# GpSimd in place of VectorE for two groups of low-part subtractions in a hybrid encoder block

## The chip, the core and the metric

The kernel runs on one core of a Trainium2 chip (trn2). The metric is the device time of one execution in microseconds (us), the median of several runs. The engines are TensorE (PE; its weight loads are listed apart as PEld), VectorE (DVE), ScalarE (ACT), GpSimd (POOL) and SyncE (SP, which here only issues DMAs). Each engine executes its own instructions in the order in which they were written into its queue.

## The reference

One layer of an encoder over 16 meta tokens and 2048 tokens of width 1024. A projection feeds two groups, attention (4 query heads, 2 key/value heads, rotary positions) and a Fourier mix; both are normalised, projected back and added, and a squared-ReLU MLP follows. What the change touches belongs to the Fourier group:

```python
def fourier_mix(u, w_f):
    b, l, _ = u.shape
    ug = u.reshape(b, l, N_FOURIER_GROUPS, FOURIER_GROUP_W)
    f = jnp.fft.fft2(ug, axes=(1, 3), norm='ortho').real
    y = jnp.einsum('blgc,gcd->blgd', f, w_f)
    return y.reshape(b, l, FOURIER_W)
...
    mixed = jnp.concatenate([rms_norm(attn, g_attn_out[i]), rms_norm(four, g_fourier_out[i])], axis=-1)
    h = h + mixed @ w_out[i]
```

## The kernel before

**Three products for one.** Nearly every large product is made of three matmuls on numbers that are split in two: `hi` is a rounded copy (written by ACT) and `lo` is what is left (`x - hi`, a subtraction on DVE). `Split` (L70 to L74) issues the two, and `mm3` (L80, L81, L82) multiplies hi by hi, hi by lo and lo by hi into one PSUM bank. So a line L70 or L71 in the profile is a split, and L80 to L82 are matmuls; the names of the tiles tell of what.

**Stages.** First the projections and their rotary and transposing work (to about 310 us), then the Fourier transform interleaved with the first attention units, then the Fourier half of the output projection interleaved with further attention units (to about 590 us), then the attention half of the output projection and the MLP with the rest of the attention.

**The Fourier transform** (`fourier`, `transform`, `load_tables`). The transform over the tokens is four products with tables of cosines and sines, `tr` 0 to 3; 0 and 1 give the even frequencies, 2 and 3 the odd ones. For each `tr`, `load_tables` (L528) loads raw tables `traw` of 128 x 516 numbers by DMA (three buffers), ACT copies each to `thi` (L548) and DVE subtracts to `tlo` (L551). The even transforms have two whole tables each, the odd ones four, so there are 12 `tlo` subtractions, 8 of them for `tr` 2 and 3. `transform` multiplies the channels by a small matrix (`pa`, L570), splits the result (`ahi`, `alo`), and its `product` makes `py`. Results are combined by DVE into two long tiles, `EV` and `UA`.

**The Fourier half of the output projection** (`out_f`). For each of 16 tiles `t` of 128 tokens, `rows(t)` gathers a tile's 128 columns from `EV` and `UA` in two interleaved halves (one tile has four pieces instead of two, so 34 pieces in all, nearly all 128 x 256 numbers, every second element of the tile): a split into `yh` and `yl` (L926, which the profile lists under L70 and L71), and a square into `ysq` on ACT (L927). GpSimd adds the squares up (`ysq`, L929, two additions a tile); `scale` sums them over the channels by a small matmul (`pys`), and DVE and GpSimd make the factor `rs_f` of it (L190, L192). Then 24 matmuls make `pof`, two banks of 12, and DVE adds each, scaled, into `xo` (L957).

**Attention beside it** (`attention`). A unit is 512 query columns. `scores` makes 17 products `s` of three matmuls; ACT copies them to tiles `S` (L773) and DVE keeps a running maximum `M` (L776, L779, L781, L768); transposes `pm_m` (L787) and `pd_m` (L796) on PE turn it into `mb`. `softmax` subtracts `mb` on DVE (L832), ACT takes the exponential (L833), DVE sums in `acc` (L837, L839) and splits each half to `ph` and `pl` (L71); PE multiplies by the values into `o`, three matmuls a split: `ph`, then `pl`, then `ph` again. The first two units multiply unsplit numbers (L842). GpSimd's queue issues the DMAs of queries `q`, keys `kt` and values `vt`.

**What sets the order.** The program is written as interleaved generators (`mix`, `with_weights`), and a scheduler then orders each engine's instructions by its own estimate of when their inputs are ready. Where an instruction moves to another engine, the order of all the others in that stretch is found anew.

Of the kernel before, what the change touches and what calls it, by code (L numbers as in the profile page):

```python
# [14 lines left out]
ALU = mybir.AluOpType  # L15
# [41 lines left out]
def f32v(ap):  # L57
    return ap.bitcast(F32)
# [18 lines left out]
def mm3(nc, out, a, b, first, last, chain=False):  # L77


    nc.tensor.matmul(out, a[0], b[0], start=first, stop=False, skip_group_check=chain)  # L80
    nc.tensor.matmul(out, a[0], b[1], start=False, stop=False, skip_group_check=chain)  # L81
    nc.tensor.matmul(out, a[1], b[0], start=False, stop=last, skip_group_check=chain)  # L82
# [53 lines left out]
def encoder_block(ctx: ExitStack, tc: tile.TileContext, x, meta, w_in, w_f,  # L136
                  w_out, w_up, w_down, g_fin, g_cols, g_rows, c_id, c_rope, c_dft, c_even, c_odd, c_rem, out):
    nc = tc.nc
    split = Split(nc)
# [9 lines left out]
    def bank(name, shape=(P, 512)):  # L149
        return mmp.tile(list(shape), F32, name=name, tag="mm")  # L150
# [36 lines left out]
    def rstd_of(pool, ss, n, width, tag, rows=P):  # L187

        ms = pool.tile([P, n], F32, name="ms_" + tag, tag="ms_" + tag, bufs=2 if pool is tp else 4)
        nc.vector.tensor_scalar(ms[:rows], ss, 1.0 / width, EPS, op0=ALU.mult, op1=ALU.add)  # L190
        rs = pool.tile([P, n], F32, name="rs_" + tag, tag="rs_" + tag, bufs=2 if pool is tp else 4)
        nc.gpsimd.tensor_tensor(rs[:rows], ms[:rows], mhalf[:rows, :n], op=ALU.pow)  # L192
        return rs
# [331 lines left out]
    def sources(tr):  # L525
        full, rest = ROWS[tr]
        return (EV, UA, EV, UA)[tr], full, rest, len(full) // 2 if tr < 2 else len(full)

    def load_tables(tr):

        src, full, rest, n_tab = sources(tr)
        rem = ft.tile([P, NG, REM], F32, name=f"rem{tr}", tag="rem", bufs=1)
        nc.vector.memset(rem, 0.0)
        for o in (0, 32, 64):
            for lo, hi in rest:
                nc.vector.tensor_copy(rem[:, :, o:o + hi - lo], src[:, :, lo:hi])
                o += hi - lo
        tabs = []
        for nt in list(range(n_tab)) + [len(full)]:
            rows = P if nt < n_tab else REM  # L540
            raw = ft.tile([P, TW], F32, name=f"traw{tr}_{nt}", tag="traw", bufs=3)
            nc.sync.dma_start(raw[:rows], (c_even[tr, nt] if tr < 2 else c_odd[tr - 2, nt]) if rows == P else c_rem[tr])
            raw = raw.rearrange("p (c n) -> p c n", c=2)
            hi = ft.tile([P, 2, CHP], R32, name=f"thi{tr}_{nt}", tag="thi", bufs=T_BUFS[1])[:, :, :CH]
            with ExitStack() as behind:
                for i in last_acts:
                    behind.enter_context(tc.issue_after(i))
                nc.scalar.copy(hi[:rows], raw[:rows])  # L548
                if rows == P:
                    lo = ft.tile([P, 2, CHP], R32, name=f"tlo{tr}_{nt}", tag="tlo", bufs=T_BUFS[0])[:, :, :CH]  # L550
                    nc.vector.tensor_tensor(lo, raw, f32v(hi), op=ALU.subtract)  # L551
                    tabs.append((hi, lo))
                else:
                    nc.vector.tensor_tensor(hi[32:64], raw[32:64], f32v(hi[32:64]), op=ALU.subtract)
                    tabs.append(hi)
        tables[tr] = tabs, rem

    def transform(tr):

        src, full, rest, n_tab = sources(tr)  # L560
        if tr not in tables:
            load_tables(tr)
# [32 lines left out]
    for j in range(LAST + 1):  # L595
# [16 lines left out]
        else:  # L612
            if j == 1:
                chan_dft()
            if j == LAST:
                for _ in proj_u(j):
                    side()
                spread_m()
                for src in (EV, UA):
                    for g in range(NG):  # L620
                        fold(src, g)
                    for g in range(0, NG, 2):
                        fold_even(src, g)
                wu.release()
                ft = Lines(tc.alloc_tile_pool(name="ft", bufs=1, reuse_waits="tile"), small)
                load_tables(0)
# [20 lines left out]
    def y_runs(par, e0, e1):  # L647

        m, t0, o0, t1, o1 = YO if par else YE
        got = []  # L650
        if e0 < m:
            got.append((t0, o0 + e0, e0, min(e1, m) - e0))
        if e1 > m:
            s = max(e0, m)
            got.append((t1, o1 + s - m, s, e1 - s))
        return got
# [40 lines left out]
    def misc(name, shape=(P, 512)):  # L697
        return app.tile(list(shape), F32, name=name, tag="misc")
# [204 lines left out]
    def weights(pool, bufs, k, h, keep):  # L903
        raw = pool.tile([P, 512], F32, name=f"wfr{k}_{h}", tag="wr", bufs=bufs)
        nc.sync.dma_start(raw, w_out[512 + k * P:512 + (k + 1) * P, h * 512:(h + 1) * 512])
        wt[k, h] = tuple(keep.tile([P, 512], R32, name=f"wf{e}{k}_{h}") for e in "hl")
        split(*wt[k, h], raw, c_fo(k))

    def out_f():
        xts, ops = {}, {}  # L910

        def load(t):
            xts[t] = op_.tile([P, D], F32, name=f"xo_{t}", tag="xo", bufs=2)
            nc.sync.dma_start(xts[t], x[t * P:(t + 1) * P, :])

        def rows(t):

            hi = op_.tile([P, NG, P], R32, name=f"yh_{t}", tag="yh", bufs=2)
            lo = op_.tile([P, NG, P], R32, name=f"yl_{t}", tag="yl", bufs=2)
            sq = op_.tile([P, NG, P], F32, name=f"ysq_{t}", tag="ysq", bufs=2)  # L920
            for par in range(2):
                for src, col, e, n in y_runs(par, 64 * t, 64 * t + 64):
                    y = src[:, :, col:col + n]
                    o = 2 * (e - 64 * t) + par
                    v = slice(o, o + 2 * n - 1, 2)
                    split(hi[:, :, v], lo[:, :, v], y)  # L926
                    nc.scalar.square(sq[:, :, v], y)  # L927
            for n in (2, 1):
                nc.gpsimd.tensor_tensor(sq[:, :n], sq[:, :n], sq[:, n:2 * n], op=ALU.add)  # L929
            ops[t] = [hi, lo, sq]  # L930

        def scale(t):
            ps = misc(f"pys_{t}", (P, 1))
            nc.tensor.matmul(ps, ops[t].pop()[:, 0], ones, start=True, stop=True)
            ops[t].append(rstd_of(op_, ps, 1, 512, "f"))

        load(0)
        rows(0)
        for k in range(NG // 2, NG):
            for h in range(2):  # L940
                weights(wp, 3, k, h, op_)
            yield
        scale(0)
        for t in range(NT):
            hi, lo, rf = ops.pop(t)
            xt = xts.pop(t)
            for h in range(2):
                ps = bank(f"pof_{t}_{h}")
                with tc.issue_after(ended[0]) if 2 * t + h >= 2 * NT - HELD else nullcontext():
                    for k in range(NG):  # L950
                        mm3(nc, ps, (hi[:, k, :], lo[:, k, :]), wt[k, h], k == 0, k == NG - 1)
                if h == 0 and t + 1 < NT:
                    rows(t + 1)
                elif t + 1 < NT:
                    scale(t + 1)
                hs = slice(h * 512, (h + 1) * 512)
                nc.vector.scalar_tensor_tensor(xt[:, hs], ps, rf, xt[:, hs], op0=ALU.mult, op1=ALU.add)  # L957
                yield
                if h == 0 and t + 1 < NT:
                    load(t + 1)  # L960
            nc.sync.dma_start(h_d[t], xt)
# [447 lines left out]
    for g in range(8):  # L1409
# [5 lines left out]
        for name in ORDER:  # L1415
            hi, lo = ready.pop(0)
# [371 lines left out]
```

## Time and profile before

| | us |
|---|---|
| median of 3 runs (2291.70 to 2292.91) | 2292.0 |
| the profiled execution | 2293.14 |
| its span, first to last instruction | 2291.4 |
| PE busy | 2278.1 (99%) |
| DVE busy | 1718.7 (75%) |
| ACT busy | 1280.6 (56%) |
| POOL busy | 184.0 (8%) |

The span is what the trace covers; the profiled execution's own time is 1.7 us more, and it lies 1.1 us over the median. An engine's busy time is the union of its instructions. Matmuls are pipelined, so that one is listed as busy while the next has begun: in a run of matmuls without a gap, those with 512 columns start 0.23 us apart although each is listed with 0.39 us. A wait of PE under about 0.15 us therefore doesn't show as a gap, and a longer one shows only in part; the distance from one matmul's start to the next shows all of it.

### The profile page before, as it was taken

To read this page: it belongs to the slowest core of one execution; us is meant where nothing else is said; L and a number is where in the kernel's file an instruction comes from. 1 tells how busy PE (TensorE), PEld (TensorE's weight loads), DVE (VectorE), ACT (ScalarE), POOL (GpSimd) and SP (SyncE) were. 2 spreads that over 40 slices of the span, in tenths; PEclk is the share of its full clock that TensorE was granted. 3 is DMA by queue.
4 is the path that set the end of the run, shared out by engine and by line. 5 is a ranking of instruction groups with operands and counts; after the bars stand their busy time and mean duration, and the time that the engine had idled before them with its cause. 6 is when DMAs were issued, how large, how long until landed. Compare 5 with 4: busy or idle time off the path is not lost.

```text
span 2291.4 us, 30005 instructions
## 1 busy us (share of the span) xinstructions
PE 2278.1 (99%) x10846; PEld 1883.0 (82%) x10846; DVE 1718.7 (75%) x2448; ACT 1280.6 (56%) x2303; POOL 184.0 (8%) x235
## 2 busy tenths in 40 slices
PE   9999999999999999999999999999999999999998
PEld 7888988777888888888888888888888888888887
DVE  6435588999986877986887877885875656697796
ACT  6443356566665655665765775664665545543344
POOL 2212120222000000000000100000000000200000
PEclk9999999999999999999999999999999999999999
DMA  6343252543533222333342453224454444865442
GB/s 213 100 119 102 78 169 79 190 137 120 166 117 108 96 87 79 114 114 106 97 157 87 157 175 104 92 82 170 140 177 158 152 152 156 303 193 165 129 138 83
DMA packets 178069, 307.23 MB, mean 134 GB/s; under 512 B 14960, under 2 KB 63728, under 8 KB 177536
## 3 DMA queue, kind: packets, MB, share of 16 engines
q1 hardware_dynamic: 159136, 262.89, 34.9%
q0 software_dynamic: 18640, 42.16, 6.2%
q8 instruction: 85, 1.39, 0.3%
q14 instruction: 64, 0.52, 0.1%
q10 hardware_dynamic: 144, 0.26, 0.0%
HBM read 225.27 MB, written 79.99 MB: 133 GB/s over the span
## 4 chain that ended last, share of the span: by engine, by line
PE 94%; DVE 3%; DMA 1%; ACT 1%; issue 1%; POOL 0%; SPq 0%; POOLq 0%; DVEq 0%; ACTq 0%
PE pdn L80 5%; PE pdn L82 5%; PE pdn L81 5%; PE pup L80 5%; PE pup L82 5%; PE pup L81 5%; PE s L80 3%; PE s L82 3%; PE s L81 3%; PE ux L80 2%; PE ux L81 2%; PE ux L82 2%; PE dx L80 2%; PE dx L82 2%; PE dx L81 2%; PE o L81 2%
## 5 line engine op out<-in xcount | busy, mean ns | idle before, releaser
L80 PE MATMUL pdn<-wh_dn,ah 128*128 128x512 f32 x512 | 201.5, 394 | 0.2 <-ACT r L1154 0.2
L80 PE MATMUL pup<-mTh,wh_up 128*128 128x512 f32 x512 | 201.5, 394 | 0.0
L81 PE MATMUL pup<-mTl,wh_up 128*128 128x512 f32 x512 | 200.7, 392 | 0.0
L82 PE MATMUL pup<-mTh,wl_up 128*128 128x512 f32 x512 | 200.4, 391 | 0.0
L81 PE MATMUL pdn<-wl_dn,ah 128*128 128x512 f32 x512 | 199.9, 390 | 0.0
L82 PE MATMUL pdn<-wh_dn,al 128*128 128x512 f32 x512 | 198.7, 391 | 0.0
L773 ACT COPY S<-s 128x512 f32<-128x512 f32 x256 | 148.4, 584 | 55.6 <-PE s L82 48.5
L70 ACT CAST wh_up<-wr_up 128x512 fp32r<-128x512 f32 x128 | 79.4, 620 | 164.3 <-PE pup L81 76.5
L832 DVE TENSOR_TENSOR S<-S,mb 128x1024 f32<-128x1024 f32 x128 | 154.8, 1218 | 8.4 <-ACT mb L803 8.2
L71 DVE TENSOR_TENSOR pl<-S,ph 128x512 fp32r<-128x512 f32 x196 | 132.3, 696 | 11.0 <-ACT ph L70 10.7
L833 ACT ACTIVATE S<-S 128x1024 f32<-128x1024 f32 x114 | 120.7, 1060 | 34.7 <-DVE S L832 34.1
L70 ACT CAST wh_dn<-wr_dn 128x512 fp32r<-128x512 f32 x128 | 79.1, 620 | 107.9 <-PE pdn L82 52.6
L71 DVE TENSOR_TENSOR wl_up<-wr_up,wh_up 128x512 fp32r<-128x512 f32 x128 | 87.6, 687 | 68.1 <-ACT wh_up L70 63.3
L839 DVE TENSOR_TENSOR acc<-acc,S 128x1024 f32<-128x1024 f32 x110 | 134.1, 1219 | 1.3 <-ACT S L833 1.1
L71 DVE TENSOR_TENSOR wl_dn<-wr_dn,wh_dn 128x512 fp32r<-128x512 f32 x128 | 87.2, 687 | 60.2 <-ACT wh_dn L70 51.8
L70 ACT CAST ph<-S 128x512 fp32r<-128x512 f32 x196 | 118.7, 620 | 15.9 <-PE o L82 12.5
L70 ACT CAST ah<-a 128x1024 fp32r<-128x1024 f32 x56 | 58.5, 1048 | 118.2 <-issue 60.8
L779 DVE TENSOR_TENSOR M<-M,S 128x1024 f32<-128x1024 f32 x96 | 118.0, 1229 | 6.7 <-ACT S L773 6.0
L80 PEld LDWEIGHTS pdn<-wh_dn,ah 128*128 128x128 f32 x512 | 96.1, 188 | 23.5 <-ACT r L1154 3.6
L80 PE MATMUL s<-q,kt 128*128 128x512 f32 (+1 forms) x272 | 113.0, 415 | 0.1
L82 PEld LDWEIGHTS pdn<-wh_dn,al 128*128 128x128 f32 x512 | 96.2, 188 | 19.9
L82 PEld LDWEIGHTS pup<-mTh,wl_up 128*128 128x128 f32 x512 | 96.2, 188 | 19.4
(345 smaller groups left out, 6413.0 us busy)
## 6 DMA issues: line engine op xcount, KB each, us to landing
wr_up<-in_w_up_dram SPq DMA_DIRECT2D x128, 256.0 KB, 2.8
wr_dn<-in_w_down_dram SPq DMA_DIRECT2D x128, 256.0 KB, 2.6
a<-s_d SPq DMA_DIRECT2D x42, 512.0 KB, 3.6
R<-in_w_up_dram SPq DMA_DIRECT2D x16, 1024.0 KB, 5.2
s_d<-s SPq DMA_DIRECT2D x64, 256.0 KB, 2.2
d<-in_w_down_dram SPq DMA_DIRECT2D x26, 512.0 KB, 5.0
s_d<-c SPq DMA_DIRECT2D x48, 256.0 KB, 2.4
x<-in_x_dram SPq DMA_DIRECT2D x16, 512.0 KB, 4.9
```

Source lines behind the costliest of these rows:

```text
L70: self.high = nc.scalar.copy(hi, src)
L71: self.low = nc.vector.tensor_tensor(lo, src, f32v(hi), op=ALU.subtract)
L80: nc.tensor.matmul(out, a[0], b[0], start=first, stop=False, skip_group_check=chain)
L81: nc.tensor.matmul(out, a[0], b[1], start=False, stop=False, skip_group_check=chain)
L82: nc.tensor.matmul(out, a[1], b[0], start=False, stop=last, skip_group_check=chain)
L773: nc.scalar.copy(S[:, i % 2], ps)
L779: nc.vector.tensor_tensor(M, M, S, op=ALU.max)
L832: nc.vector.tensor_tensor(S, S, mb, op=ALU.subtract)
L833: nc.scalar.activation(p, S, AF.Exp, scale=ISQ)
L839: nc.vector.tensor_tensor(acc, acc, p, op=ALU.add)
```

## The change

For `tr` 2 and 3 the subtraction that makes `tlo` is issued to GpSimd instead of DVE, and in `rows` the one that makes `yl` likewise, in all 34 pieces. Sizes, buffers and what is computed stay.

```diff
@@ load_tables
                 if rows == P:
                     lo = ft.tile([P, 2, CHP], R32, name=f"tlo{tr}_{nt}", tag="tlo", bufs=T_BUFS[0])[:, :, :CH]
-                    nc.vector.tensor_tensor(lo, raw, f32v(hi), op=ALU.subtract)
+                    (nc.vector if tr < 2 else nc.gpsimd).tensor_tensor(lo, raw, f32v(hi), op=ALU.subtract)
                     tabs.append((hi, lo))
@@ rows
-                    split(hi[:, :, v], lo[:, :, v], y)
+                    nc.scalar.copy(hi[:, :, v], y)
+                    nc.gpsimd.tensor_tensor(lo[:, :, v], y, f32v(hi[:, :, v]), op=ALU.subtract)
                     nc.scalar.square(sq[:, :, v], y)
```

The lines behind the second place move down by one. On every engine the order is the same as before up to the tables of `tr` 2 and again from about 610 us on; between them instructions have moved on all engines. PE issues the same matmuls. On DVE 42 instructions are gone, on POOL there are 42 more.

GpSimd's queue at the tables, behind the last DMA that it issues for the first attention units (`q_3644` is a query tile, `kt_1_...` the next units' keys):

```order
 L726 DMA vm_0_3642<-v_m 96x128
 L744 DMA q_3644<-q_d_103 128x2x512
+L551 TENSOR_TENSOR tlo_0_3918<-traw_0_3914,thi_0_3916 128x2x258
+L551 TENSOR_TENSOR tlo_1_3924<-traw_1_3920,thi_1_3922 128x2x258
+L551 TENSOR_TENSOR tlo_2_3930<-traw_2_3926,thi_2_3928 128x2x258
+L551 TENSOR_TENSOR tlo_3_3936<-traw_3_3932,thi_3_3934 128x2x258
 L711 DMA kt_1_0_4383<-k_d 128x2x512
+L551 TENSOR_TENSOR tlo_0_4237<-traw_0_4233,thi_0_4235 128x2x258
 L711 DMA kt_1_1_4385<-k_d 128x2x512
```

The four subtractions of `tr` 2 now stand ahead of the load of the next keys, and the first of `tr` 3 ahead of the one after. On ACT the fourth `thi` of `tr` 2 (`thi_3_3934`) has moved as well: it stood behind the eighth copy and exponential after `mb`, and now stands between the first exponential, of `S_0`, and the second, of `S_2`.

PE's queue in the middle of the output projection, at an attention unit's products (`ph_11_0`, `pl_11_0` are the two parts of one half tile of exponentials):

```order
 L80 MATMUL o_4885<-ph_11_0_5173,vt_1_2_4395 128x512
+L81 MATMUL o_4885<-pl_11_0_5174,vt_1_2_4395 128x512
+L82 MATMUL o_4885<-ph_11_0_5173,vt_1_2_4395 128x512
+L80 MATMUL o_4885<-ph_11_1_5180,vt_1_2_4395 128x512
+L81 MATMUL o_4885<-pl_11_1_5181,vt_1_2_4395 128x512
+L82 MATMUL o_4885<-ph_11_1_5180,vt_1_2_4395 128x512
 L80 MATMUL s_9_5187<-q_4914,kt_1_2_4387 128x512
 L81 MATMUL s_9_5187<-q_4914,kt_1_2_4387 128x512
```

Before, nine other matmuls (`s_9`, `s_10` and three of `pof`) stood between the first `o` and the one that reads `pl_11_0`; now none does. Of the 24 such pairs of `ph` and `pl` in the three units of this stretch, 15 had other matmuls between them before, 98 in all; now 7 have, 47 in all.

GpSimd's queue where the query tile of a later attention unit is loaded (`q_5473`), before:

```order
L192 TENSOR_TENSOR rs_f<-ms_f,mhalf 128x1
L929 TENSOR_TENSOR ysq_5412<-ysq_5412 128x256
L929 TENSOR_TENSOR ysq_5412<-ysq_5412 128x128
L744 DMA q_5473<-q_d_104 128x2x512
L192 TENSOR_TENSOR rs_f<-ms_f,mhalf 128x1
```

And now:

```order
L192 TENSOR_TENSOR rs_f<-ms_f,mhalf 128x1
L930 TENSOR_TENSOR ysq_5412<-ysq_5412 128x256
L930 TENSOR_TENSOR ysq_5412<-ysq_5412 128x128
L927 TENSOR_TENSOR yl_5411<-UA,yh_5410 128x256 x2
L744 DMA q_5473<-q_d_104 128x2x512
L192 TENSOR_TENSOR rs_f<-ms_f,mhalf 128x1
```

Two subtractions of a tile's `yl` stand ahead of the load.

## Rows read from the trace of the kernel before

**Rows 1.** The page, busy time of each engine.
```profile
PE 2278.1 (99%) x10846; PEld 1883.0 (82%) x10846; DVE 1718.7 (75%) x2448; ACT 1280.6 (56%) x2303; POOL 184.0 (8%) x235
```
**Rows 2.** Busy time by stretch: PE, PEld, DVE, ACT, POOL (instructions), PEclk, DMA, GB/s.
```profile
340.00:420.00 80.00, 79.65 (x477) 64.01 (x476) 73.68 (x108) 45.78 (x76) 4.29 (x6) 1.00 0.30 85
420.00:590.00 170.00, 168.50 (x755) 131.91 (x754) 163.06 (x230) 104.54 (x199) 45.26 (x56) 1.00 0.50 164
```
**Rows 3.** PE's waits from 340 to 600 us: us in total, times, longest.
```profile
PE o L81 <- DVE pl L71: 0.8, 3, 0.4
PE pm_m L787 <- DVE M L768: 0.4, 1, 0.4
PE py L590 <- DVE ahi L581: 0.2, 1, 0.2
```
**Rows 4.** Groups of DVE, 420 to 590 us: busy us, mean ns | idle before.
```profile
L957 DVE SCALAR_TENSOR_TENSOR xo<-pof,rs_f,xo 128x512 f32<-128x512 f32 x32 | 23.7, 741 | 1.8 <-PE pof L82 1.5
L779 DVE TENSOR_TENSOR M<-M,S 128x1024 f32<-128x1024 f32 x18 | 22.9, 1271 | 0.0
L71 DVE TENSOR_TENSOR pl<-S,ph 128x512 fp32r<-128x512 f32 x32 | 22.7, 740 | 0.0
L71 DVE TENSOR_TENSOR yl<-EV,yh 128x256 fp32r<-128x256 f32 x14 | 7.6, 586 | 0.1
L71 DVE TENSOR_TENSOR yl<-UA,yh 128x256 fp32r<-128x256 f32 x16 | 6.1, 415 | 0.0
```
**Rows 5.** The tile tlo on DVE, whole run: ns min/median/max, first and last start.
```profile
L551 DVE TENSOR_TENSOR tlo<-traw,thi x12: 632/692/699, 285.3 to 389.4; 128x516 fp32r<-128x516 f32 x12
```
**Rows 6.** Timelines of POOL and DVE at 421 us: start, us, engine, line, operation.
```profile
421.22 1.15 POOL L929 TENSOR_TENSOR ysq<-ysq 128x256 f32<-128x256 f32 x1
421.70 1.75 DVE L779 TENSOR_TENSOR M<-M,S 128x1024 f32<-128x1024 f32 x1
```
**Rows 7.** Timelines of POOL and DVE at 551 us.
```profile
551.16 0.74 POOL L929 TENSOR_TENSOR ysq<-ysq 128x256 f32<-128x256 f32 x1 [1.03 <-ACT ysq L927]
551.21 1.23 DVE L71 TENSOR_TENSOR pl<-S,ph 128x512 fp32r<-128x512 f32 x1
```
**Rows 8.** Timelines of POOL, DVE and PE, 331 to 343 us.
```profile
330.98 0.73 POOL L744 DMA_DIRECT2D q<-q_d  x1
332.85 7.87 DVE L779 TENSOR_TENSOR M<-M,S 128x1024 f32<-128x1024 f32 x6
342.02 0.68 DVE L768 TENSOR_TENSOR M<-M,S 96x512 f32<-96x512 f32 x1
342.76 0.44 PE L787 MATMUL pm_m<-ident,M 128*128 128x128 f32 x2
```
**Rows 9.** Timeline of ACT, 346 to 357 us: three exponentials, and a thi.
```profile
346.77 3.39 ACT L833 ACTIVATE S<-S 128x1024 f32<-128x1024 f32 x3 [1.29 <-DVE S L832]
...
355.96 0.63 ACT L548 CAST thi<-traw 128x516 fp32r<-128x516 f32 x1
```
**Rows 10.** Timelines of POOL and PE at the first tile of the output projection.
```profile
421.22 2.55 POOL L929 TENSOR_TENSOR ysq<-ysq 128x256 f32<-128x256 f32 x2
424.35 0.28 PE L934 MATMUL pys<-ones,ysq 128*128 128x1 f32 x2
```
**Rows 11.** Timeline of PE at 470 us.
```profile
470.23 0.39 PE L80 MATMUL pof<-wfh,yh 128*128 128x512 f32 x1
470.91 0.50 PE L81 MATMUL o<-pl,vt 128*128 128x512 f32 x1 [0.29 <-DVE pl L71]
```
**Rows 12.** Timelines of POOL, ACT and PE at 508 us, and the query tile's landing.
```profile
507.76 0.73 ACT L70 CAST yh<-UA 128x256 fp32r<-128x256 f32 x2 [1.91 <-PE pof L81]
509.25 0.76 POOL L744 DMA_DIRECT2D q<-q_d  x1 [4.95 <-PE s L82]
DMA to landing us min/median/max: 6.5/6.5/6.5
515.76 0.50 PE L80 MATMUL s<-q,kt 128*128 128x512 f32 x1
```

## The prediction

> **What bounds the kernel now.** Busy time comes first [rows 1]: PE is busy for 2278.1 us of a span of 2291.4, so 13.3 us in all are left to win by waiting less, and the change adds and removes no matmul. Only where DVE makes PE wait can a lighter DVE pay. The busy time by stretch shows where that could be [rows 2]: while PE has no gap to speak of, DVE is busy for 73.68 of 80 us (92%) beside the odd transforms and for 163.06 of 170 (96%) beside the Fourier half of the output projection. So DVE is close to being the bound there, yet PE waited for it with a visible gap only a few times [rows 3]: three times for `pl`, 0.8 us, once for `M`, once for `ahi`. Gaps understate it. Where PE waited for `pl` at 470 us, two matmuls start 0.68 us apart instead of 0.23 [rows 11], so 0.45 us were lost there and 0.29 are shown. Counted so, the three waits are worth some 1.4 us, and what could be won by all of DVE's relief is about 2 us.
>
> **What is taken off DVE.** The 34 pieces of `yl`: the 16 whole ones of `UA` take 415 ns each, the 14 of `EV` 586 [rows 4]. With 415 ns for each, 34 x 0.415 = 14.1 us, and 14 x 0.171 = 2.4 us of stretching, 16.5 us in all. The 8 `tlo` at 692 ns [rows 5] are 5.5 us. If that were all, DVE would be busy for 86% of the output projection's stretch.
>
> **What it gets back.** GpSimd's additions already run there, and they show the price. One of 128 x 256 alone takes 0.74 us [rows 7]. The `pl` that DVE starts 0.05 us behind it takes 1.23 us, where the group's mean, stretched ones among it, is 0.74 [rows 4, 7]. The same at 421 us: POOL's addition starts at 421.22, the `M` behind it takes 1.75 us, against a mean of 1.271 [rows 4, 6]. So a DVE instruction that reads two tiles of SBUF and meets one of POOL's loses about 0.5 us to each 256 numbers; and POOL's own addition stretches to 1.15 us, as it waits for DVE's. `xo`, which reads PSUM, shows no such thing: a mean of 741 ns [rows 4]. It makes up 23.7 of the 163 us; with the pieces that find DVE idle I take two thirds of the moved pieces to meet a DVE instruction that they hold up. That gives 34 x 0.5 x 2/3 = 11.3 us, for the 14.1 + 2.4 taken off. A `tlo` has 516 numbers; by proportion it takes POOL 0.74 x 516/256 = 1.5 us and costs DVE 1.0 us where they meet: 8 x 1.0 x 2/3 = 5.3 us for 5.5. So DVE is lighter by about 5 us of 250 and stays above 90% busy: what was moved away mostly comes back as waiting.
>
> The Trainium skill, "SBUF — State Buffer", section "Who interferes with whom", says that a VectorE instruction with two inputs in SBUF and a GpSimd instruction that reads SBUF exclude each other, and that the later one is blocked until the first has finished. The rows show 0.5 us of POOL's 0.74, so the trace agrees in kind and not in size; by the whole duration, the return would be 34 x 0.74 x 2/3 = 16.8 us, more than what was taken off. What that would do is the first rival.
>
> **What moves with it, and the sum.** The scheduler's new order has been shown at three places; it supposes an earlier DVE, and PE's queue is strict, so DVE's lateness becomes a wait of PE. Terms, positive for slower:
>
> 1. *Tables of `tr` 2.* POOL can start the three subtractions when its query DMA is issued, at 331.71 [rows 8]. They fall on the six `M` of the first unit, which took 7.87 us for 6 x 1.23 of work, so they were nearly back to back, and the last `M` ended at 342.70, 0.06 us before PE's transposes that read it [rows 8]. Three meetings cost 3 x 1.0 us; the three `tlo` taken off give 2.1 us, but the `M` can't run ahead of their scores by that much. Bounds 0 and +3.0; I take +1.2, nearer to the first because half of the 2.1 us should count.
> 2. *`thi` on ACT.* A cast of 0.63 us now stands between the first exponential and the second, which had run without a gap, three in 3.39 us [rows 9]; PE's `o` matmuls wait for each. Bounds 0 (it fits behind) and +1.0 (it waits for its buffer too); +0.5.
> 3. *Tables of `tr` 3.* DVE had three `tlo` ahead of its last `M`; PE waited 0.2 us for the `ahi` behind them [rows 3]. Bounds -0.4 (all of it, hidden part included) and +0.5; -0.2.
> 4. *First tile.* POOL's two additions ended at 423.77, and PE's `pys` that reads their sum started at 424.35 [rows 10], 0.58 us later. Now two subtractions of at least 0.74 us stand ahead in the queue. One fits into earlier idle time. Bounds 0 and +1.5; +0.3.
> 5. *The `pl` products.* PE reads `pl` nine matmuls (9 x 0.23 = 2.1 us) sooner at the place shown, 51 matmuls fewer in between over all 24 pairs. DVE's real lead is 5 us spread over 250, the order's is 22. Eight pairs lost their cover; if each waits as that at 470 us did, 8 x 0.45 = 3.6 us, and 4.5 with the pairs before them; if the lead holds, the old 1.4 us go. Bounds -1.4 and +4.5; +1.0, as DVE's load and so its lag behind POOL are about what they were while the cover is halved.
> 6. *Query tile.* Its DMA was issued at 509.25, landed 6.5 us later and PE's `s` started at 515.76, at once [rows 12]. Two `yl` now stand ahead, ready when ACT ends their casts at 508.49: POOL is done between 509.6 (0.74 each from the first cast's end on) and 510.9 (stretched). Bounds 0 and +1.7; +0.7.
>
> Covered by slack and costed at nothing: the later `yl` itself (it is made for the tile after the one that PE works on, half a tile or some 170/16/2 = 5 us ahead, and POOL is busy for 45 of 170 us [rows 2]); the later `kt` loads, whose tiles serve units to come; `rs_f`, short and due half a tile later. If POOL's queue fell behind by those 5 us, PE would wait for `yl` at every tile.
>
> The sum is 1.2 + 0.5 - 0.2 + 0.3 + 1.0 + 0.7 = +3.5 us. Against the profiled execution of 2293.14 that is 2296.6; this execution lies 1.1 us over the median of the runs, so for the median I write 2292.0 + 3.5 = 2295.5. The lower bounds sum to -1.8, the upper to +12.2.
>
> **The rivals.** A measurement of this kernel tells about 0.2% from no change, 4.6 us here.
>
> *The lock decides, slower.* If a meeting costs DVE POOL's whole 0.74 us (1.5 for a `tlo`) and nearly every piece meets one, the return is 34 x 0.74 = 25.2 us against 16.5: the output projection's stretch would ask 163.06 + 8.7 = 171.8 us of DVE in 170. The point from which it decides is a DVE that is asked for more than its stretch, or loses its lead at each hoisted `pl`: then 1.8 us of overrun, the 4.5 of term 5 and some 2 to 4 of terms 1, 2 and 6 make +8 to +10, so 2297 to 2302. For it: DVE at 96% with two-input work nearly throughout, and an order that was planned for less. Against it: the rows give 0.5, not 0.74. This is what the rule named above gives if taken whole.
>
> *The relief holds.* POOL's pieces meet DVE when it is idle or reads PSUM, and PE's waits for DVE go: the lower bounds, -1.8, so 2290.2, and hardly a gain of 0.2%, as PE has no more to win there. For it: POOL is idle for three quarters of the time. Against it: DVE has 4% of idle time to meet.
>
> *Nothing of it is felt.* Every term at nothing, 2292: the two effects cancel on DVE and the new order is as well covered as the old one.
>
> **How the numbers follow.** My forecast, a loss between 0.5 and 4.6 us, has 0.42; the lock deciding, above 4.6 us, 0.38; relief or nothing felt, between -4.6 and +0.5, 0.17; a gain above 4.6 us, by something that the rows don't show, 0.03. So the chances are 0.03 for faster by over 0.2%, 0.42 + 0.17 = 0.59 for within it, and 0.38 for slower. The range for 8 times in 10 goes from 2290.5, near the lower bounds, to 2301, most of the lock's.
>
> **What would show it.** In the profile after: DVE's busy time from 420 to 590 us should fall by 3 to 8 us only, not by 16; the `M`, `S` and `pl` groups should have higher means (`M` above 1.35 us); POOL's `yl` should take 0.74 to 1.3 us and its busy time grow by 35 to 50 us. PE's waits should list `pl`, the `M` at 343 us and the query tile with a few tenths to 1.5 us each. If the means of DVE's groups stay as they are, the price of a meeting is wrong; if PE waits for `yl`, `rs_f` or `kt`, the slack is; if a single new wait exceeds 4 us, the terms are. A time under 2290 would mean that DVE's load was holding PE in a way that its gaps don't show.

## The result, and the profile after

The changed kernel takes 2303.79 us (median of 6 runs, 2303.18 to 2304.86) and the one before, on the same chip, 2292.26 (6 runs, 2291.70 to 2293.28): the ratio is 1.0050, interval 1.0040 to 1.0061, so 11.5 us slower. The forecast was 2295.5 with a range up to 2301.

Where the time went shows when the n-th matmul of TensorE starts in one trace and in the other (PE issues the same number in both):

| time before, us | PE later after the change, us |
|---|---|
| 340 | 0.0 |
| 350 | 5.8 |
| 360 to 390 | 6.4 |
| 400 to 420 | 7.8 |
| 430 | 8.4 |
| 450 | 8.9 |
| 510 to 520 | 8.0 |
| 560 | 11.9 |
| 590 and on, to 1900 | 11.5 |

Two thirds came by 400 us, in the tables of `tr` 2 and 3, and the other third in the output projection. (The spans, 2302.0 and 2291.4, differ by only 10.6: the profiled execution before lost 0.8 us of its own behind 1900 us.)

Busy time on the page, as in [rows 1]:

```profile
PE 2281.2 (99%) x10846; PEld 1885.4 (82%) x10846; DVE 1718.1 (75%) x2406; ACT 1279.5 (56%) x2303; POOL 249.7 (11%) x277
```

42 instructions have left DVE, and its busy time is what it was, 1718.1 us now and 1718.7 before; POOL's grew by 65.7 us. By stretch, as in [rows 2] (busy us of PE, PEld, DVE, ACT, POOL, then PEclk, DMA, GB/s):

```profile
342.00:350.00 8.00, 3.34 (x15) 3.00 (x15) 7.28 (x14) 0.00 (x0) 0.00 (x0) 0.68 0.00 0
350.00:360.00 10.00, 10.00 (x45) 6.96 (x44) 8.00 (x11) 5.35 (x8) 1.45 (x1) 0.91 0.10 26
340.00:420.00 80.00, 74.20 (x436) 60.21 (x436) 70.00 (x96) 40.98 (x68) 11.39 (x11) 0.96 0.27 80
420.00:590.00 170.00, 164.93 (x740) 128.13 (x739) 157.21 (x189) 103.20 (x200) 96.00 (x88) 1.00 0.44 146
427.74:601.47 173.73, 168.66 (x755) 132.01 (x754) 159.54 (x195) 103.88 (x199) 97.01 (x90) 1.00 0.47 157
```

The last line is the stretch that holds the matmuls of 420 to 590 us before. PE was without a gap to speak of before [rows 2]; now it stands still for more than half of 342 to 350 us, and the granted clock falls. Its waits, as in [rows 3], 340 to 600 us:

```profile
PE pm_m L787 <- DVE M L768: 5.7, 2, 4.7
PE o L81 <- DVE pl L71: 3.5, 6, 1.0
PE py L80 <- DVE alo L576: 0.5, 1, 0.5
PE pa L570 <- DVE alo L576: 0.5, 1, 0.5
PE pys L935 <- POOL ysq L930: 0.3, 1, 0.3
PE py L590 <- DVE ahi L581: 0.2, 1, 0.2
```

**The largest wait.** DVE's timeline in the place of [rows 8] (start, duration, then what ran):

```profile
331.42 5.56 DVE L776 TENSOR_TENSOR M<-S,S 128x1024 f32<-128x1024 f32 x1 [1.90 <-ACT S L773]
337.08 7.87 DVE L779 TENSOR_TENSOR M<-M,S 128x1024 f32<-128x1024 f32 x6
```

And POOL's, there:

```profile
331.61 0.73 POOL L744 DMA_DIRECT2D q<-q_d  x1
332.36 3.52 POOL L551 TENSOR_TENSOR tlo<-traw,thi 128x516 fp32r<-128x516 f32 x3
```

The first `M`, 1.23 us of work, is recorded for 5.56: it ends 1.1 us behind the third `tlo`. The six `M` behind it take the same 7.87 us as before and so end 4.2 us late. PE's timeline shows what that did:

```profile
346.99 1.11 PE L787 MATMUL pm_m<-ident,M 128*128 128x128 f32 x4 [4.66 <-DVE M L768]
...
349.19 0.63 PE L80 MATMUL s<-q,kt 128*128 128x512 f32 x1
349.62 0.63 PE L81 MATMUL s<-q,kt 128*128 128x512 f32 x1
350.04 0.63 PE L82 MATMUL s<-q,kt 128*128 128x512 f32 x1
```

The transposes start at 346.99 instead of 342.76 [rows 8]. Behind the pause the matmuls of 512 columns start 0.43 us apart where they started 0.23 apart: PE runs at the lower level of its clock, 1.2 GHz, until about 351.5. In the measure of the table PE is 4.4 us late at 343 and 6.4 at 346 (transposes and `py` at the lower clock too) and stays so, so the pause cost 4.4 us and the clock behind it some 1.9 more.

**The small waits.** Groups of DVE from 420 to 590 us, as in [rows 4]:

```profile
L832 DVE TENSOR_TENSOR S<-S,mb 128x1024 f32<-128x1024 f32 x22 | 28.2, 1300 | 1.5 <-ACT mb L803 1.5
L779 DVE TENSOR_TENSOR M<-M,S 128x1024 f32<-128x1024 f32 x18 | 25.4, 1409 | 3.4 <-ACT S L773 3.4
L71 DVE TENSOR_TENSOR pl<-S,ph 128x512 fp32r<-128x512 f32 x28 | 21.8, 809 | 0.0
L958 DVE SCALAR_TENSOR_TENSOR xo<-pof,rs_f,xo 128x512 f32<-128x512 f32 x28 | 20.7, 741 | 4.3 <-PE pof L82 4.2
```

`M` went from 1271 to 1409 and `pl` from 740 to 809, while `xo`, which reads PSUM, stayed at 741. One meeting in detail, POOL's and DVE's timelines at 551 us:

```profile
550.71 1.73 POOL L927 TENSOR_TENSOR yl<-UA,yh 128x256 fp32r<-128x256 f32 x1
552.39 1.72 POOL L930 TENSOR_TENSOR ysq<-ysq 128x256 f32<-128x256 f32 x1
```

```profile
550.09 1.73 DVE L779 TENSOR_TENSOR M<-M,S 128x1024 f32<-128x1024 f32 x1
551.75 1.77 DVE L839 TENSOR_TENSOR acc<-acc,S 128x1024 f32<-128x1024 f32 x1
553.44 1.22 DVE L71 TENSOR_TENSOR pl<-S,ph 128x512 fp32r<-128x512 f32 x1
```

They take turns: `yl` (0.75 us alone) waits until `M` has ended at 551.82, `acc` until `yl` has at 552.43, and so on. A held DVE instruction ends 1.08 us behind POOL's where it takes 1.22 alone, or 0.55 where 0.69: so it waits for the whole of what is left of POOL's, and 0.14 us of its own front part runs meanwhile. Added up over `M`, `S`, `acc`, `pl` and `wfl` between 418 and 600 us (each one's duration less the shortest of its kind and shape, where the rest is over 0.06 us), 12 instructions were held for 4.4 us before, and 37 for 16.2 us now.

### The profile page after: what moved, and what is told of

It is laid out like the page before. It is cut to its first block, busy times and chain, and to the rows that moved or that the text cites. A ratio compares the mean times of both kernels' runs of the same rounds, so it can differ in the third digit from the quotient of the medians.

```text
span 2302.0 us, 30026 instructions
## 1 busy us (share of the span) xinstructions
PE 2281.2 (99%) x10846; PEld 1885.4 (82%) x10846; DVE 1718.1 (75%) x2406; ACT 1279.5 (56%) x2303; POOL 249.7 (11%) x277
## 4 chain that ended last, share of the span: by engine, by line
PE 95%; DVE 3%; issue 1%; ACT 1%; POOL 1%; POOLq 0%; DVEq 0%; ACTq 0%
PE pdn L80 5%; PE pdn L82 5%; PE pdn L81 5%; PE pup L80 5%; PE pup L82 5%; PE pup L81 5%; PE ux L80 3%; PE ux L81 3%; PE ux L82 3%; PE dx L80 2%; PE dx L81 2%; PE dx L82 2%; PE s L80 2%; PE s L82 2%; PE s L81 2%; PE o L81 2%
## 5 line engine op out<-in xcount | busy, mean ns | idle before, releaser
L832 DVE TENSOR_TENSOR S<-S,mb 128x1024 f32<-128x1024 f32 x128 | 156.5, 1233 | 10.6 <-ACT mb L803 10.4
L70 ACT CAST ph<-S 128x512 fp32r<-128x512 f32 x196 | 118.6, 619 | 12.7 <-PE o L82 9.5
```

The lines of the kernel that those rows point to most:

```text
L70: self.high = nc.scalar.copy(hi, src)
L832: nc.vector.tensor_tensor(S, S, mb, op=ALU.subtract)
```

## Experiments

Times of before differ by some tenths between batches; each ratio is against the runs of before on the same chip. Theory L says that DVE's waiting for POOL is the cause; theory O that the moved order is, whatever POOL does.

**One part at a time.** The tables alone (the diff's first place, without its second):

> Only the tables of tr 2 and 3 go to GpSimd; the channels' low parts stay on VectorE. From 420 us on the program is the old one. In the changed kernel's trace TensorE's lag behind the old one grew by 6.4 us between 340 and 360 us and by 1.3 more by 400 us, so 7.8 of 11.5 us before any channel was moved. Theory L (a VectorE instruction with two inputs in SBUF that meets GpSimd's is held until GpSimd's has ended, and the hold lands on the chain of M): 7 to 8.5 us slower than before, 2299 to 2301, with the 5.6 us first M, the wait for M at 343 us of 4.5 to 5 us, and a granted clock under 1 behind it. Rival A (the two parts add to each other, and the tables alone are cheap): under 4 us, below 2296.

2299.80 us, ratio 1.0032 (1.0019 to 1.0044), +7.5. The two largest waits, 330 to 600 us:

```profile
PE pm_m L787 <- DVE M L768: 5.2, 2, 4.8
PE o L81 <- DVE pl L71: 0.8, 3, 0.4
```

PE is 6.5 us late at 370 and 7.8 at 410, as in the change, and no later from there on. The channels alone (the second place, without the first):

> Only the channels' low parts yl go to GpSimd; the tables stay on VectorE. Theory L: the lag that came between 420 and 590 us in the changed kernel, 3 to 4 us, all of it as small waits for pl and M; 2294.5 to 2296.5, granted clock 1.00 throughout, the wait for M at 343 us back at 0.4 us. Rival A: the part after 420 us was hurt by being late from the tables, and alone costs nothing: 2291.5 to 2292.5.

2296.57, 1.0019 (1.0010 to 1.0028), +4.3. The largest waits:

```profile
PE o L81 <- DVE pl L71: 3.6, 7, 0.9
PE pm_m L787 <- DVE M L768: 1.4, 2, 1.0
PE pys L935 <- POOL ysq L930: 0.3, 1, 0.3
```

The two add up to 11.8 of 11.5, so nothing shows that they depend on each other. The odd tables of `tr` 3 alone:

```diff
-                    nc.vector.tensor_tensor(lo, raw, f32v(hi), op=ALU.subtract)
+                    (nc.vector if tr != 3 else nc.gpsimd).tensor_tensor(lo, raw, f32v(hi), op=ALU.subtract)
```

> Only the tables of tr 3 go to GpSimd; TensorE's and ScalarE's order is word for word that of before, VectorE's lacks four instructions. Theory L: the lag of 1.3 us that came between 390 and 400 us in the change, by M L779 and L781 held behind the second and third tlo and the alo behind them: 2293 to 2294. Rival (term 3 of the prediction: relief of VectorE there): 2291.5 to 2292.3.

2295.15, 1.0012 (1.0003 to 1.0022), +2.7 and over the 2293 to 2294 expected; the interval holds 0.7 to 5.0 us. The trace is sharper: PE falls 1.29 us behind between 390 and 410 us, as expected of that place, and 1.0 of it is left at 590. The rest of the 2.7 comes later, and what makes it isn't shown. In the trace of the change the same place shows why. POOL, then DVE:

```profile
395.90 3.32 POOL L551 TENSOR_TENSOR tlo<-traw,thi 128x516 fp32r<-128x516 f32 x2
```

```profile
396.48 1.69 DVE L779 TENSOR_TENSOR M<-M,S 128x1024 f32<-128x1024 f32 x1 [3.51 <-ACT S L773]
398.20 1.56 DVE L781 TENSOR_TENSOR M<-M 128x512 f32<-128x512 f32 x1
```

DVE had been idle for 3.51 us just before; the `tlo` came to POOL when the `M` came to DVE, and two were held, 0.5 and 0.9 us. The `alo` of [rows 3]'s transform stand behind them on DVE, and PE waits for two.

**The dose, with the order kept.** POOL subtracts only two columns of each group of a piece (`min(n, 2)`), half of them (`(n + 1) // 2` in its place), or all of them twice; the order on PE, DVE and ACT is that of the channels alone in all of them. In the first two the rest of `yl` stays zero, which leaves out that part of the products. The main lines of the first, against the channels alone:

```diff
-                    nc.gpsimd.tensor_tensor(lo[:, :, v], y, f32v(hi[:, :, v]), op=ALU.subtract)
+                    v2 = slice(o, o + 2 * min(n, 2) - 1, 2)
+                    nc.gpsimd.tensor_tensor(lo[:, :, v2], y[:, :, :min(n, 2)], f32v(hi[:, :, v2]), op=ALU.subtract)
```

> As the kernel with the channels alone, with the same order on TensorE, VectorE and ScalarE, but GpSimd subtracts only the first two columns of each group of a piece (8 numbers a partition in place of 256); the rest of the low part is left at zero in two tiles that are cleared once. So VectorE is free of yl as in the change, the products are as hoisted as in the change, and GpSimd hardly meets VectorE. Theory L: 2291 to 2292.5, the means of pl, M and S back at 0.69, 1.22 and 1.21 us but for the squares' additions. Theory O: the hoisted products wait whatever GpSimd does: 2294.5 to 2296.5 like the channels alone.

> As the kernel in which GpSimd subtracts only two columns of each piece, here with half of each piece (128 numbers a partition); the other half of the low part stays zero. Order on the other engines is the same. The time was 2292.1 with next to nothing and 2296.6 with all 256. Theory L (VectorE waits for the whole of GpSimd's instruction and then starts from the front): the loss grows faster than the number, as small waits hide behind the lead of VectorE first: 2292.5 to 2294. Rival (a fixed price for each meeting, whatever its length): near 2296, as with all.

> As the kernel with the channels alone, with each subtraction of yl issued twice on GpSimd, the second repeating the first; the order on the other engines is the same. Nothing cost -0.1 us, half 1.3, all 4.3. Theory L (VectorE waits out GpSimd's instruction, and its lead is used up): VectorE is held some 34 x 0.5 x 2/3 = 11 us more, which no lead covers any longer: 8 to 16 us slower than before, 2300 to 2308, the waits for pl, M and S growing. Rival (the moved order costs a fixed amount, or GpSimd's second pieces fall into VectorE's idle time): 2296 to 2298.

| POOL's subtraction of `yl` | us | ratio, interval | against before | DVE held, as counted above |
|---|---|---|---|---|
| two columns | 2292.12 | 0.9998, 0.9989 to 1.0007 | -0.1 | 19 times, 7.8 us |
| half | 2293.57 | 1.0005, 0.9996 to 1.0015 | +1.1 | 34, 12.7 |
| all (the channels alone) | 2296.57 | 1.0019, 1.0010 to 1.0028 | +4.3 | 36, 16.0 |
| all, twice | 2309.20 | 1.0072, 1.0055 to 1.0089 | +16.5 | 51, 22.4 |

Theory O falls: with the hoisted products and small subtractions nothing is lost. The holding isn't gone there (7.8 us for 4.4 before, nearly all by the squares' additions), but DVE is rid of `yl`, 15.7 us in the trace before. The largest waits, and two of DVE's groups, with two columns:

```profile
PE pm_m L787 <- DVE M L768: 1.1, 2, 0.7
PE pys L936 <- POOL ysq L931: 0.7, 1, 0.7
PE o L81 <- DVE pl L71: 0.7, 3, 0.3
```

```profile
L71 DVE TENSOR_TENSOR pl<-S,ph 128x512 fp32r<-128x512 f32 x32 | 22.7, 741 | 0.0
L779 DVE TENSOR_TENSOR M<-M,S 128x1024 f32<-128x1024 f32 x18 | 22.5, 1248 | 5.0 <-ACT S L773 5.0
```

The loss grows faster than the dose, which fits small holds that hide behind DVE's lead. Twice cost 16.5, half a microsecond over the 8 to 16 expected, and not by holding alone: DVE was held for 6.4 us more than with all, and lost was 12.2 more. POOL itself came late there, for PE's `pys` at the first tile and for the `rs_f` that DVE's `xo` needs. PE's three largest waits, and DVE's largest:

```profile
PE o L81 <- DVE pl L71: 5.9, 7, 1.8
PE pys L936 <- POOL ysq L931: 2.6, 1, 2.6
PE pm_m L787 <- DVE M L768: 2.3, 3, 1.1
DVE xo L959 <- POOL rs_f L192: 5.8, 5, 1.9
```

This series also tells what the channels could have won in this order of instructions: with nearly all of `yl`'s work off DVE and hardly any on POOL, the time is that of before.

**Moving the tables of `tr` 2 away from the `M` chain.** First by the schedule alone:

```diff
+                    with tc.issue_after(LAST_M[0]) if tr == 2 else nullcontext():
+                        (nc.vector if tr < 2 else nc.gpsimd).tensor_tensor(lo, raw, f32v(hi), op=ALU.subtract)
```

> The whole change, with the four subtractions of tr 2 held back on GpSimd until the last M of the first unit has been issued; the order on TensorE, VectorE and ScalarE is word for word that of the change. Theory L: the M chain runs as before, TensorE doesn't stop at 343 us and its clock stays at 1.00; the three tlo then meet what VectorE does behind the M (pieces of EV and UA, which read PSUM, and then three S less mb), which may cost 0 to 2.5 us: 2297 to 2300. Theory O (it is the new order of the other engines that costs the time, not the meeting): as the change, 2303 to 2304.5.

2304.54, 1.0053 (1.0041 to 1.0066), as the change; but it isn't evidence for theory O. `issue_after` orders the program and makes no engine wait for another. The order came out as the change's on POOL too, so this is the change once more: POOL began the `tlo` at 332.57, and the first `M` took 5.55 us again. So a real wait was put in: POOL adds a column of the finished `M` (here `LAST_M[0]`) first.

```diff
+                    if (tr, nt) == (2, 0):
+                        gate = ft.tile([P, 1], F32, name="gate", tag="gate", bufs=1)
+                        GATE.append(ins_of(nc.gpsimd.tensor_tensor(gate, LAST_M[0][:, :1], LAST_M[0][:, :1], op=ALU.add)))
+                    with tc.issue_after(GATE[0]) if tr == 2 else nullcontext():
+                        (nc.vector if tr < 2 else nc.gpsimd).tensor_tensor(lo, raw, f32v(hi), op=ALU.subtract)
```

> The whole change, and ahead of the four subtractions of tr 2 on GpSimd one addition of a single column that reads the finished M of the first unit, so that GpSimd really waits for it (holding them back in the schedule alone didn't move them). Theory L: the M chain ends near 342.7 us as before, TensorE has no stop at 343 us and its granted clock stays at 1.00; the tlo run from about 343 to 346.5 us beside pieces of EV and UA and meet the first S less mb, which costs 0.5 to 1.5 us in place of 6.4: 2297.5 to 2299.5. Rival: the tables come late for the products of tr 2 or hold the three S less mb one after the other: 3 us or more there, over 2300.5.

2298.32, 1.0026 (1.0016 to 1.0037), +5.9: half of the loss is gone by a wait on POOL, with the order of PE, DVE and ACT word for word the change's. POOL's timeline, and the stretches of before:

```profile
342.61 0.18 POOL L557 TENSOR_TENSOR gate<-M 128x1 f32<-128x1 f32 x1 [10.93 <-DVE M L776]
342.77 3.50 POOL L559 TENSOR_TENSOR tlo<-traw,thi 128x516 fp32r<-128x516 f32 x3
```

```profile
342.00:350.00 8.00, 7.43 (x50) 6.05 (x50) 7.39 (x13) 3.20 (x5) 4.62 (x5) 1.00 0.34 91
350.00:360.00 10.00, 10.00 (x39) 6.29 (x38) 9.98 (x14) 7.04 (x11) 1.42 (x2) 1.00 0.31 80
```

PE has no stop of microseconds any more, its clock stays at 1.00, and it is 0.4 us late at 370 instead of 6.4. The 4.4 us of pause and the 1.9 of clock are both the meeting's.

**Why one `M` was held for three `tlo`.** Elsewhere the two engines take turns, and a DVE instruction that has begun first is not held (counted below); this `M` had begun 0.94 us ahead of the first `tlo` by the records. Two versions of the change: a subtraction of a single column behind the query's DMA and ahead of the `tlo`, and the same on a column of the sixth score's tile, which comes about a microsecond later.

```diff
+                    if (tr, nt) == (2, 0):
+                        gate = ft.tile([P, 1], F32, name="gate", tag="gate", bufs=1)
+                        GATE.append(ins_of(nc.gpsimd.tensor_tensor(gate, raw[:, 0, :1], f32v(hi)[:, 0, :1], op=ALU.subtract)))
```

> The whole change, and ahead of the four subtractions of tr 2 one subtraction of a single column, behind the query's DMA. The first M of the change began 0.94 us ahead of the first tlo and yet ended only behind the third; elsewhere a VectorE instruction that has begun first is not held, and gets its turn behind each of GpSimd's. Theory D (an instruction of GpSimd's that stands right behind its DMA issues takes the tiles' port ahead of its recorded start): the small one takes that place, the first M ends near 332.7 us, the three tlo then take turns with the next M and delay each by about 1.05 us, the wait for M at 343 us is 3 to 4 us in place of 4.7, and the time 2302 to 2303. Rival R (three long ones in a row keep VectorE out whatever stands ahead): M of 5.5 us again, 2303.3 to 2304.3.

2304.03, 1.0053 (1.0036 to 1.0070). DVE, then POOL:

```profile
331.29 5.21 DVE L783 TENSOR_TENSOR M<-S,S 128x1024 f32<-128x1024 f32 x1 [1.67 <-ACT S L780]
```

```profile
331.01 0.73 POOL L751 DMA_DIRECT2D q<-q_d  x1
331.76 0.20 POOL L556 TENSOR_TENSOR gate<-traw,thi 128x1 f32<-128x1 f32 x1
331.91 3.50 POOL L558 TENSOR_TENSOR tlo<-traw,thi 128x516 fp32r<-128x516 f32 x3
```

Theory D missed here: the small one didn't take the blow, `M` was held to the end of the third `tlo` again. Only the wait for `M`, 3.9 us, lay where it had put it; PE is 6.3 us late at 370, as in the change.

```diff
+            if u == 0 and i == 5:
+                gate = ap2.tile([P, 1], F32, name="gate", tag="gate", bufs=1)
+                GATE.append(ins_of(nc.gpsimd.tensor_tensor(gate, S[:, 1, :1], S[:, 1, :1], op=ALU.add)))
```

> The whole change, and ahead of the four subtractions of tr 2 on GpSimd an addition of a single column of the sixth score's tile, so that GpSimd's queue has been idle for about a microsecond behind the query's DMA issue when the three tlo begin, near 333.3 us, still in the middle of the M chain. Theory D (what keeps VectorE out for three in a row is that they stand right behind GpSimd's DMA issues): the first M takes 1.2 us, the three tlo take turns with the following M, three of which take about 2.3 us; the M chain ends some 3 us late, the wait for M at 343 us is 2.8 to 3.8 us in place of 4.7: 2302 to 2303. Rival R (three long ones in a row keep VectorE out anyway): one M of over 4.5 us, the wait 4.5 us or more, 2303.3 to 2304.3.

2301.35, 1.0038 (1.0023 to 1.0053). DVE, then POOL:

```profile
331.09 1.23 DVE L783 TENSOR_TENSOR M<-S,S 128x1024 f32<-128x1024 f32 x1 [1.67 <-ACT S L777]
332.59 10.46 DVE L786 TENSOR_TENSOR M<-M,S 128x1024 f32<-128x1024 f32 x6 [0.28 <-ACT S L777]
```

```profile
331.28 0.73 POOL L748 DMA_DIRECT2D q<-q_d  x1
332.65 1.22 POOL L780 TENSOR_TENSOR gate<-S 128x1 f32<-128x1 f32 x1 [0.64 <-ACT S L777]
333.83 5.48 POOL L555 TENSOR_TENSOR tlo<-traw,thi 128x516 fp32r<-128x516 f32 x3
```

With 0.64 us of idle time between the DMA issue and the rest, three of the six `M` take turns with the `tlo` (10.46 for 7.87: 0.86 each). The wait for `M` is 2.7 us, just under the 2.8 to 3.8 of theory D, the time is 0.7 us under its 2302 to 2303, and the clock's mean in 342 to 350 us is 0.79 in place of 0.68. So three long ones in a row don't keep DVE out. That the first `M` isn't held proves less: it had ended 0.3 us before POOL's next instruction began. The second had begun 0.06 us ahead of that one and wasn't held.

So the DMA issue right ahead is suspected. One kernel with a pause doesn't settle it, as its `tlo` also came 1.5 us later and behind another instruction; a count over all twelve traces says more. It takes the DVE instructions with two inputs in SBUF that had begun over 0.05 us ahead of POOL's and had over 0.2 us left. Where POOL's stood elsewhere, none of 266 was held over 0.1 us (two `wl` at 31 us, begun 0.02 and 0.03 us ahead, were). Where it stood right behind a DMA issue, 11 were held, among them an `M` at 457 us in the change, for 0.96 us, and, in the kernel with half pieces, a `wfl` that waited out two `yl` and a `ysq`, 1.58 us. But 17 were not: in each of the twelve an `M` ahead of a one-column `rs_m` (at 1304.32 us in the trace before), and five others, among them an `S` at 420.56 in the trace before, begun 0.1 us into the issue. A DMA issue alone held none of the 97 such DVE instructions that overlapped one in the trace before. So a DMA issue right ahead went with every such hold, but doesn't always bring one. What POOL does in that time, the traces don't show, and it stays open.

## Why the prediction was wrong

The sum had the right sign, but the time was out of the range by 2.8 us, and the loss that came, over 4.6 us, had 0.38 of the chances where 0.59 went to a time within 4.6 us of before. By its own steps:

- *DVE's relief and return.* The kind was right, the size only in part. The held time grew by 11.8 us where 11.3 was worked out. The sign named for it, 3 to 8 us less of DVE from 420 to 590 us, came true with 5.9, partly by luck: PE is late there, so the same window holds 740 matmuls in place of 755. For the same matmuls (the last stretch shown) DVE is busy for 159.5 us in place of 163.1, and together with those from 340 us on for 236.9 in place of 236.7. So over both stretches DVE was not lighter by 5 us but by nothing. POOL's busy time grew by 50.7 us from 420 to 590 and by 65.7 in all, for 35 to 50. The reading of the rule under it was off. The Trainium skill, "SBUF — State Buffer", section "Who interferes with whom", says that the later one is blocked until the first has finished; the prediction took 0.5 of 0.74 us for a disagreement. Where DVE came second, the timelines agree with the rule: it waits out all that is left, and 0.14 us of its own start is hidden in it. The 11 holds behind a DMA issue don't agree: by the records DVE's instruction came first there.
- *Term 1, tables of `tr` 2: this step failed.* +1.2, bounds 0 and +3.0; measured +6.4. It supposed that `M` and `tlo` take turns, and took half of the `tlo`'s 2.1 us off again. In the change DVE got no turn, and the pause was 4.4 us. And it priced a pause as its length: the clock behind it, 1.9 us more, was in no term. Even with turns, in the kernel with 0.64 us behind the DMA issue, PE is 3.9 us late, still over the bound: 2.3 at 343 us and 1.6 more behind that pause, where the clock was at 0.79. The bound should have held at least the whole of POOL's three, 3.5 us (1.2 each, not the 1.5 taken by proportion), on a chain that [rows 8] showed with 0.06 us to spare.
- *Term 2, `thi` on ACT.* +0.5; nothing to be seen: PE's lag is 6.4 us from 352 to 390.
- *Term 3, tables of `tr` 3.* -0.2, bounds -0.4 and +0.5; measured +1.3. It took [rows 3]'s wait for `ahi` as something that a lighter DVE relieves (it is 0.2 us as before), and didn't ask when POOL's `tlo` would run: at the moment when the last `M` came, as ACT casts the tables just then.
- *Term 4, first tile.* +0.3; PE fell 0.6 us behind there. Within its bounds.
- *Term 5, the `pl` products.* +1.0, bounds -1.4 and +4.5; from 430 to 590 us PE fell back by 3.1 us, the regained 0.9 between 490 and 510 in it. Mechanism and bounds right, the size taken too low: `M` at 458 us was late too, and eight matmuls on `pl` started 0.2 to 1.1 us late.
- *Term 6, query tile.* +0.7; none, but narrowly. The tile landed at 523.70 and PE's `s` began at 523.80 without a gap; in four of the other kernels PE waited 0.2 to 0.9 us for a query tile.

The terms as measured sum to 6.4 + 1.3 + 0.6 + 3.1 = 11.4. The upper bounds summed to +12.2, close to what came, but by other terms. The rival on the other side, that the lock decides, gave 2297 to 2302 and was nearer than the forecast (its own +8 to +10 makes 2300 to 2302). The lock was nearly as whole as it said; its place, a DVE asked for more than its stretch, wasn't the cause (DVE is busy for 157 of 170 us). The sign named for the terms being wrong, a single new wait over 4 us, is what the profile showed.

## What to carry to other kernels

Moving a two-input VectorE instruction to GpSimd takes away its duration and gives back what is left of GpSimd's wherever the two meet; what was free of it here was VectorE's `xo`, which reads PSUM. None of these kernels gained by the move. So ask of each moved instruction *when* it will run and which chain stands on VectorE then, not how busy the engines are on average. Where it must go, a data dependence can hold it behind the critical chain, which an order of issue alone didn't; keep it off the heels of GpSimd's own DMA issues where that costs nothing; and to any stop of TensorE of some microseconds add the slower clock behind it.

## What the runs showed of the hardware that was not expected

- A GpSimd instruction right behind a DMA issue of GpSimd's can keep out a VectorE instruction that was recorded as begun up to 0.94 us earlier (11 of 28 times), and those that follow it without a pause do so too: 4.3 us in one piece. With 0.64 us of idle time in between, the two engines took turns.
- The granted clock was 0.68 on average in the 8 us that hold a pause of 4.7 us, 0.79 with one of 2.7, and 1.00 where PE didn't stop; behind the long pause it took until 351.5, some 4.5 us, before `py` matmuls were 0.12 us apart as before.
- An addition of a single column on GpSimd took 0.18 us alone and 1.22 where a VectorE `M` was running: so a small one waited as well. Right behind a DMA issue it took 0.20 us, although an `M` was recorded as begun.
